# Low parts of 36 weights made by an accumulating transfer instead of a subtraction on VectorE

## The chip, the cores and the metric

The kernel runs on one core of a Trainium2 chip. The metric is the device time of one execution in microseconds; the median of three runs of the kernel before is 1605.04 us (1604.93 to 1605.2). TensorE multiplies, VectorE and ScalarE do elementwise work, GpSimd (POOL in the profile) does some of it too, and SyncE (SP) issues the transfers. Each engine works through its own instructions in order.

## The reference

One layer of an encoder, applied to two sequences of 512 tokens, model width 1024. In outline:

```python
def _layer(x, mem, l, p):
    xn = _rmsnorm(x, p['norm_mix'][l])
    mn = _rmsnorm(mem, p['norm_mem'][l])
    h = xn @ p['w_in'][l]
    u, q, k, v, xq, g = jnp.split(h, IN_SPLITS, axis=-1)
    y_s5 = _s5_branch(u, ...)                       # state-space recurrence, both directions, then a GLU
    y_diff = _diff_attention(rope(q), rope(k), v, lam, ...)
    y_x = _cross_attention(xq, mk, mv)              # mk, mv = split(mn @ w_mem_kv)
    branches = (y_s5, y_diff, y_x)
    merged = sum(sigmoid(g[..., n]) * (branches[n] @ p['w_up'][l, n]) for n in range(3))
    x = x + merged @ p['w_out'][l]
    xn2 = _rmsnorm(x, p['norm_ffn'][l])
    gate, up = jnp.split(xn2 @ p['w_ffn_in'][l], 2, axis=-1)
    return x + (silu(gate) * up) @ p['w_ffn_out'][l]
```

The columns of `w_in` are, in tiles of 128: 4 for `u`, 4 for `q`, 4 for `k`, 4 for `v`, 4 for `xq`, and 24 for the three gates `g` (8 each).

## The kernel before

**Products.** Operands are float32 numbers split in two: a high part rounded to fp32r and a low part, what is left of it. A product is three matmuls, high by high, high by low and low by high, accumulated in one PSUM bank (`mm3`, L153). A weight tile is 128 output columns by 1024 inputs, held as 128 partitions by 1024 elements (512 KB). For both sequences it is used in 2 x 8 x 3 = 48 matmuls of 512 columns each.

**A weight's way.** `weight` (L143) loads the tile to `wf`, then calls `split` (L131): ScalarE copies `wf` to `wh`, which rounds it, and VectorE subtracts `wh` from `wf` and writes `wl`. The pool `wp` (L83) has two buffers each of `wf`, `wh` and `wl`. So the load of a weight waits until the split of the weight two places earlier has read its `wf`, and the split waits until TensorE has finished with the `wh` and `wl` of the weight two places earlier.

**Who calls it.** `proj` (L163) multiplies a whole weight tile at once. It makes 18 of the 24 gates (`gates`, L402; three calls with the counts in `NG`, L42, and single ones between the steps of the recurrence) and the GLU's four products, whose weights are half as long (`nk` is 4). `units` (L614) is the same as a generator that gives control back every six matmuls; it makes the other six gates (`gate_units`, L627), the four queries to the memory (`xq_units`, L661), four queries and four keys of the differential attention (`qk_units`, L763, and one in the list at L686), and the merge's products, again with half-size weights. The values come from `v_units` (L637), which holds two weights at once and uses them in turn until its end.

**Order.** First the memory's keys and values and the norms; then the four `u` weights; then gates, which fill TensorE while S5's operands are made and while the recurrence runs on VectorE (`s5_gen`, L1410; `next(s5)` runs it a stretch further); the GLU; then attention on the memory, and the differential attention. In both attentions TensorE's order is the program's own (`PE.on`, L687): `fill` (L598) takes projections from a list (L686, L828) and puts their matmuls between the scores and the outputs. Then the merge, the output product, and the feed-forward part with its own weight preparation. Weights for the last product are prepared during the attentions: POOL makes sums of raw tiles (`raw_sums`, L451), ScalarE and VectorE split them, and SP stores them. In the rotation of queries and keys (`rotated`, L745) POOL has two of the steps. Outside the stretches with `PE.on`, and on the other engines, a planner orders each engine's instructions by a simulated time line (L1788). Three kinds of edges guide it without a wait at run time: `queued` puts transfers behind the last weight load (`last_w`), `behind` puts matmuls behind the last one (`last_mm`), and `issue_after(last_s[...])` puts VectorE's or ScalarE's instructions behind the last split of a weight (`last_s`); the last is used for the recurrence's stretches between the gates.

Of the kernel before, what the change touches and what calls it, by code (L numbers as in the profile page):

```python
# [10 lines left out]
F32 = mybir.dt.float32  # L11
F32R = mybir.dt.float32r
I32 = mybir.dt.int32
AF = mybir.ActivationFunctionType
ALU = mybir.AluOpType
# [4 lines left out]
P = 128  # L20
L = 512
DM = 1024
KD = DM // P
# [49 lines left out]
def encoder(ctx: ExitStack, tc: tile.TileContext, a, out):  # L73
    nc = tc.nc
    V, S, PO, PE = nc.vector, nc.scalar, nc.gpsimd, InOrder(tc, nc.tensor)
# [30 lines left out]
    def slot(tag, shape=(P, NT), dt=F32, name="sl"):  # L106
        return pools[tag].tile(list(shape), dt, tag=tag, name=name)

    def bank(tag="mm"):
        return pools[tag].tile([P, 512], F32, tag=tag, name="bk" + tag)  # L110
# [20 lines left out]
    def split(hi, lo, src, scale=None):  # L131

        if scale is None:
            h = S.copy(hi, src)  # L134
            l_ = V.tensor_tensor(out=lo, in0=src, in1=hi.bitcast(F32), op=ALU.subtract)  # L135
        else:
            h = S.activation(out=hi, in_=src, func=AF.Copy, scale=scale)
            l_ = V.scalar_tensor_tensor(out=lo, in0=src, scalar=scale, in1=hi.bitcast(F32), op0=ALU.mult, op1=ALU.subtract)
        return h, l_

    last_w = last_s = None

    def weight(src, n=DM, tag=None):  # L143
        nonlocal last_w, last_s
        wf = wp.tile([P, DM], F32, tag="wf", name="wf")
        last_w = nc.sync.dma_start(wf[:, :n], src)
        wh, wl = (slot(tag, dt=F32R, name=n_) if tag else wp.tile([P, DM], F32R, tag=n_, name=n_) for n_ in ("wh", "wl"))
        last_s = split(wh[:, :n], wl[:, :n], wf[:, :n])
        return wh, wl

    last_mm = None
# [1 line left out]
    def mm3(outs, wh, wl, xs, k, nk):  # L153

        nonlocal last_mm
        ws = slice(k * P, (k + 1) * P)
        for s, (xh, xl) in enumerate(xs):
            PE.matmul(outs[s], wh[:, ws], xh, start=(k == 0), stop=False)
            PE.matmul(outs[s], wh[:, ws], xl, start=False, stop=False)
        for s, (xh, xl) in enumerate(xs):  # L160
            last_mm = PE.matmul(outs[s], wl[:, ws], xh, start=False, stop=(k == nk - 1))

    def proj(src, hi, lo, nk=KD, seqs=(0, 1)):  # L163


        wh, wl = weight(src, nk * P)
        outs = []
        for s in seqs:
            cs = slice(s * L, (s + 1) * L)
            outs.append(bank())  # L170
            for k in range(nk):
                mm3(outs[-1:], wh, wl, [(hi[k][:, cs], lo[k][:, cs])], k, nk)
        return outs
# [135 lines left out]
    wf = wp.tile([P, DM], F32, tag="wf", name="wf")  # L309
    wh, wl = (wp.tile([P, DM], F32R, tag=n_, name=n_) for n_ in ("wh", "wl"))  # L310
# [6 lines left out]
    mem_part(2)  # L317
    mem_part(3)
    mw.append(weight(a["w_mk"][1]))
    with queued():  # L320
        nc.sync.dma_start(ident, a["ident"])
    mem_k(0, mw[0])
    mw.append(weight(a["w_mk"][2]))
    with queued():
        next(s5)
# [76 lines left out]
    def gates(n):  # L402

        for _ in range(n):
            t = next(todo)
            o = proj(a["w_in"][20 + t], xh, xl)
            gt = slot("ld", name="gt")
            for s in range(NS):
                cs = slice(s * L, (s + 1) * L)
                S.activation(out=gt[:, cs], in_=o[s], func=AF.Tanh, scale=0.5)  # L410
            nc.sync.dma_start(gD[t], gt)
# [113 lines left out]
    for t in range(4):  # L525
        o = proj(a["w_glu"][t], zh, zl, 4)
        sg = slot("zt", name="sg")
        for s in range(NS):
            S.activation(out=sg[:, s * L : (s + 1) * L], in_=o[s], func=AF.Tanh, scale=0.5, bias=bh[:, t : t + 1])
        for s in range(NS):  # L530
            g_ = sg[:, s * L : (s + 1) * L].rearrange("p (j c) -> p j c", j=T)
            V.scalar_tensor_tensor(out=g_, in0=g_, scalar=1.0, in1=zs[t][:, :, s, :], op0=ALU.add, op1=ALU.mult)
        nc.sync.dma_start(bD[0, t], sg)
# [79 lines left out]

    def units(src, hi, lo, use, nk=KD):  # L614

        wh, wl = weight(src, nk * P)
        for s in range(NS):
            cs = slice(s * L, (s + 1) * L)
            o = bank()
            for k in range(nk):  # L620
                mm3([o], wh, wl, [(hi[k][:, cs], lo[k][:, cs])], k, nk)
                if k == nk - 1:
                    use(s, o)
                if k % 2 == 1:
                    yield 6

    def gate_units():  # L627
        t = next(todo)
        gt = slot("ld", name="gt")

        def use(s, o):
            S.activation(out=gt[:, s * L : (s + 1) * L], in_=o, func=AF.Tanh, scale=0.5)

        yield from units(a["w_in"][20 + t], xh, xl, use)
        nc.sync.dma_start(gD[t], gt)
# [25 lines left out]
    def xq_units(h):  # L661
        def use(s, o):
            qs[h, s] = tuple(xa.tile([P, L], F32R, tag=n_, name=n_, bufs=3) for n_ in ("qh", "ql"))
            qs_in[:] = split(*qs[h, s], o)

        return units(a["w_in"][16 + h], xh, xl, use)
# [17 lines left out]
    V.tensor_tensor(out=nlam, in0=nlam, in1=le[:, 0:1], op=ALU.subtract)  # L684
    xq = {h: xq_units(h) for h in range(1, 4)}
    queue += [xq[1], gate_units(), xq[2], xq[3], v_units(0, v0), gate_units(), units(a["w_in"][4], xh, xl, dq0.__setitem__)]  # L686
    PE.on = True  # L687
    steps = [(h, s, lt) for h in range(4) for s in range(NS) for lt in range(4)]
# [214 lines left out]
    n = len(steps)  # L903
# [342 lines left out]
    for v, (m, lo_, hi_) in enumerate(VISITS):  # L1246
        ps = [bank() for _ in range(6)] + [aux()]
        for p in range(lo_, hi_):
# [12 lines left out]
            for p_, (nm, o) in zip(ps, SEVEN):  # L1261
                wh, wl = w[nm]
# [529 lines left out]
```

## Time and profile before

| what | us |
|---|---|
| median of the runs | 1605.04 (1604.93 to 1605.2) |
| profiled execution, span | 1603.0 |
| TensorE (PE) busy | 1587.1, 99% of the span |
| VectorE (DVE) busy | 1162.9, 73% |
| ScalarE (ACT) busy | 640.0, 40% |
| GpSimd (POOL) busy | 541.6, 34% |
| `wl<-wf,wh` on VectorE, all weights | 145.1 (134 instructions) |

The profile is of one execution. It gives the span from the first to the last instruction, 1603.0 us; a run's time as a whole isn't given beside it, and the median of the runs is 2.0 us longer. In rows of the time line the first number is the start in us from the span's start, the second the duration in us, then the engine, the line and the instruction with its tiles, and in brackets how long the engine stood idle before it and who released it. Matmuls overlap: each has a duration of about 0.39 us in the records, but in a steady run one starts every 0.23 us. So the time that 48 of them take is read from starts, not from durations.

The stages lie in the span as follows: `u` weights 50 to 97 us; gates beside S5 97 to 337, with the recurrence from 162 to 262; GLU to 371; both attentions to 706; merge, output and feed-forward to the end.

### The profile page before, as it was taken

Reading aid. Unit: us, or ns where it says so; the run is one execution under the profiler, and the core shown is the slowest. Engines: PE = TensorE matmul, PEld = TensorE weight load, DVE = VectorE, ACT = ScalarE, POOL = GpSimd, SP = SyncE. Lnnn points to the kernel's source line nnn. Section 1 sums busy time; section 2 is a strip of 40 time slices with the busy share of each in tenths; the row PEclk is TensorE's granted clock in tenths of the full one; section 3 lists DMA queues with packets and bytes.
Section 4 is the critical chain, followed back from the end, with each engine's and each line's share of the span. In section 5 each row is a group of like instructions: output and inputs, shape, how many; then the busy total and the mean of one; then the engine's idle time right before and its main releaser. Section 6 shows DMA issues by size and latency. Waiting matters only on the chain.

```text
span 1603.0 us, 21625 instructions
## 1 busy us (share of the span) xinstructions
PE 1587.1 (99%) x7838; PEld 1314.8 (82%) x7838; DVE 1162.9 (73%) x1856; ACT 640.0 (40%) x1142; POOL 541.6 (34%) x449
## 2 busy tenths in 40 slices
PE   9999999999999999999999999999999999999997
PEld 7888788888898778778878878888888888788877
DVE  7976996076773766776465678888898778988654
ACT  6544323274652455574133443332333323233323
POOL 0010100001333220300343367676665553444653
PEclk9999999999999999999999999999999999999998
DMA  9554523576762111244454432333323223986222
GB/s 366 173 160 150 179 95 125 180 273 201 252 224 102 54 47 40 73 156 140 145 190 132 144 118 80 131 119 129 121 106 118 79 88 119 344 332 198 80 66 106
DMA packets 104891, 237.86 MB, mean 148 GB/s; under 512 B 13520, under 2 KB 45008, under 8 KB 104784
## 3 DMA queue, kind: packets, MB, share of 16 engines
q1 hardware_dynamic: 104784, 236.47, 43.1%
q8 instruction: 62, 1.02, 0.3%
q14 instruction: 45, 0.37, 0.1%
HBM read 165.16 MB, written 71.27 MB: 147 GB/s over the span
## 4 chain that ended last, share of the span: by engine, by line
PE 87%; issue 4%; DVE 3%; DMA 3%; POOL 2%; ACT 0%; SPq 0%; POOLq 0%; DVEq 0%; ACTq 0%
PE bkmm L66 75%; PE bksc L66 3%; PE bktr L66 2%; PE bkoo L66 2%; PE bktr L69 2%; DVE tl L135 1%; PE bktr L1626 1%; POOL mg L793 1%; PE bktr L1597 1%; DMA yt<-bD 1%; PE bktr L1686 0%; PE bktr L1687 0%; PE bktr L1685 0%; PE bktr L1565 0%; DMA acc<-in_w_fo 0%
## 5 line engine op out<-in xcount | busy, mean ns | idle before, releaser
L66 PE MATMUL bkmm<-xh,wh 128*128 128x512 f32 x640 | 255.4, 399 | 0.0
L66 PE MATMUL bkmm<-xh,wl 128*128 128x512 f32 x640 | 250.9, 392 | 0.0
L66 PE MATMUL bkmm<-xl,wh 128*128 128x512 f32 x640 | 250.5, 391 | 0.0
L66 PE MATMUL bkmm<-tl,wh 128*128 128x512 f32 (+1 forms) x621 | 241.2, 388 | 1.4 <-DVE tl L135 1.4
L66 PE MATMUL bkmm<-th,wl 128*128 128x512 f32 (+1 forms) x621 | 241.0, 389 | 0.9 <-DVE wl L135 0.9
L66 PE MATMUL bkmm<-th,wh 128*128 128x512 f32 (+1 forms) x621 | 241.1, 389 | 0.0
L134 ACT CAST wh<-wf 128x1024 fp32r<-128x1024 f32 (+1 forms) x134 | 117.9, 880 | 224.1 <-PE bkmm L66 179.8
L135 DVE TENSOR_TENSOR wl<-wf,wh 128x1024 fp32r<-128x1024 f32 (+1 forms) x134 | 145.1, 1083 | 50.2 <-ACT wh L134 45.7
L66 PEld LDWEIGHTS bkmm<-xh,wh 128*128 128x128 f32 x640 | 120.3, 188 | 30.3 <-issue 7.9
L66 PE MATMUL bkmm<-th,w 128*128 128x512 f32 x432 | 141.5, 392 | 2.7 <-DVE up L1101 1.0
L66 PEld LDWEIGHTS bkmm<-xh,wl 128*128 128x128 f32 x640 | 120.2, 188 | 26.7 <-issue 1.3
L66 PEld LDWEIGHTS bkmm<-xl,wh 128*128 128x128 f32 x640 | 120.4, 188 | 22.4 <-issue 0.4
L66 PEld LDWEIGHTS bkmm<-tl,wh 128*128 128x128 f32 x621 | 116.6, 188 | 25.9 <-DVE tl L135 2.1
L66 PEld LDWEIGHTS bkmm<-th,wl 128*128 128x128 f32 x621 | 116.5, 188 | 25.7 <-DVE wl L135 1.7
L66 PEld LDWEIGHTS bkmm<-th,wh 128*128 128x128 f32 x621 | 116.6, 188 | 23.9
L1165 POOL TENSOR_TENSOR up<-up,acc 128x512 f32<-128x512 f32 x44 | 83.6, 1920 | 87.8 <-DVE up L1101 87.8
L454 POOL TENSOR_TENSOR raw<-raw 128x128 f32<-128x128 f32 x28 | 15.2, 545 | 284.4 <-DVE nb L545 206.5
L66 PEld LDWEIGHTS bkmm<-th,w 128*128 128x128 f32 x432 | 80.9, 188 | 23.8 <-DVE up L1101 3.4
L793 POOL TENSOR_TENSOR mg<-mg,gl 128x1024 f32<-128x1024 f32 x16 | 43.5, 2720 | 139.0 <-DVE gl L789 139.0
L548 ACT ACTIVATE e<-bksc,nb 128x512 f32<-128x512 f32 (+1 forms) x96 | 58.8, 615 | 73.5 <-DVE nb L543 51.9
L66 PE MATMUL bkmm<-tl,w 128*128 128x512 f32 x216 | 84.2, 390 | 0.0
L66 PE MATMUL bkmm<-yh,wh 128*128 128x512 f32 x192 | 75.9, 397 | 0.8 <-ACT wh L134 0.4
(641 smaller groups left out, 3527.8 us busy)
## 6 DMA issues: line engine op xcount, KB each, us to landing
wf<-in_w_in SPq DMA_DIRECT2D x40, 512.0 KB, 3.9
wD<-hl SPq DMA_DIRECT2D x28, 512.0 KB, 2.9
w<-wD SPq DMA_DIRECT2D x28, 512.0 KB, 5.0
gD<-gt SPq DMA_DIRECT2D x24, 512.0 KB, 2.8
gl<-gD SPq DMA_DIRECT2D x24, 512.0 KB, 3.4
wf<-in_w_fg SPq DMA_DIRECT2D x22, 512.0 KB, 3.7
wf<-in_w_fu SPq DMA_DIRECT2D x22, 512.0 KB, 3.6
aD<-ac SPq DMA_DIRECT2D x22, 512.0 KB, 3.1
```

Of the source, the lines that this page charges most:

```text
L66: return self.put(self.eng.matmul(*args, **kw))
L69: return self.put(self.eng.transpose(*args, **kw))
L134: h = S.copy(hi, src)
L135: l_ = V.tensor_tensor(out=lo, in0=src, in1=hi.bitcast(F32), op=ALU.subtract)
L454: PO.tensor_tensor(out=a22, in0=a21, in1=a22, op=ALU.add)
L548: last_x = S.activation(out=e, in_=sc, func=AF.Exp, bias=nb, scale=scale, accum_out=sm)
L793: PO.tensor_tensor(out=mg[m], in0=mg[m], in1=gt, op=ALU.add)
L1165: PO.tensor_tensor(out=up, in0=up, in1=accs[s], op=ALU.mult)
L1597: PE.matmul(kp[64 * hf : 64 * hf + 48, g * 144 : (g + 1) * 144], l_[:, 2 * hf + g, :], o_[:, 4 * g4 + 2 * hf + g, :], start=(l_ is lr48), ...
L1626: PE.matmul(ps[:, g * P : (g + 1) * P], w_[:, gg * P : (gg + 1) * P], u_[:, 8 * o + gg, :], start=True, stop=True)
```

## The change

A second way to split, `split_by_transfer`, is used for whole-length weights in `proj` and in `units`: 24 gates, four queries to the memory, four queries and four keys, 36 in all. ScalarE writes `wh` as before, and in a second pass writes the negated, rounded weight to `wl`. Then POOL issues a transfer that adds `wf` onto `wl` in place, reading and writing `wl` as float32. VectorE has no part in it. The four `u` weights, the values, the GLU's and the merge's weights are split as before. For the 36, `last_s` isn't set any more and stays at the last weight split in the old way.

```diff
+    def split_by_transfer(hi, lo, src):
+
+        S.copy(hi, src)
+        S.activation(out=lo, in_=src, func=AF.Copy, scale=-1.0)
+        return PO.dma_start(lo.bitcast(F32), src, accum_op=ALU.add)
+
     last_w = last_s = None
 
-    def weight(src, n=DM, tag=None):
+    def weight(src, n=DM, tag=None, far=False):
...
-        last_s = split(wh[:, :n], wl[:, :n], wf[:, :n])
+        if far:
+            split_by_transfer(wh, wl, wf)
+        else:
+            last_s = split(wh[:, :n], wl[:, :n], wf[:, :n])
         return wh, wl
...
     def proj(src, hi, lo, nk=KD, seqs=(0, 1)):
 
 
-        wh, wl = weight(src, nk * P)
+        wh, wl = weight(src, nk * P, far=nk == KD)
...
     def units(src, hi, lo, use, nk=KD):
 
-        wh, wl = weight(src, nk * P)
+        wh, wl = weight(src, nk * P, far=nk == KD)
```

## The prediction

> **What bounds the kernel now.** I read the core list first, then busy time and slices on the page, TensorE's waits, the windows by stage, and last the time line around each weight.
>
> ```profile
> core 0: 1603.0 us, clock 0.997
> PE 1587.1 (99%) x7838; PEld 1314.8 (82%) x7838; DVE 1162.9 (73%) x1856; ACT 640.0 (40%) x1142; POOL 541.6 (34%) x449
> ...
> 182.00:262.00 80.00, 80.00 (x370) 65.51 (x370) 76.70 (x212) 18.04 (x31) 0.50 (x2) 1.00 0.37 129
> 371.00:706.00 335.00, 335.00 (x1899) 277.50 (x1898) 226.13 (x484) 175.75 (x405) 80.98 (x96) 1.00 0.34 120
> 706.00:1603.00 897.00, 883.06 (x4043) 729.09 (x4041) 668.42 (x812) 301.63 (x447) 444.53 (x324) 0.99 0.42 141
> ```
>
> TensorE is the bound: busy 99% of the span at a granted clock of 0.997. In the windows (length, then busy time of PE, PEld, DVE, ACT, POOL, then clock, DMA share and GB/s) it is busy for the whole of the recurrence's 80 us and of attention's 335 us. The 36 weights of the change are cast between 97 and 671 us, all inside stretches of that kind. Asked who TensorE waited for between 42 and 706 us, the trace gives no row; over the whole span its longest are these:
>
> ```profile
> PE bkmm L66 <- DVE tl L135: 1.4, 2, 0.8
> ...
> PE bkmm L66 <- DVE up L1101: 1.0, 2, 0.7
> PE bkmm L66 <- DVE wl L135: 0.9, 1, 0.9
> ```
>
> So nothing that VectorE gives up in these stages can shorten them: there is no idle time of TensorE to remove. What the change can do is make TensorE wait, so the question is how late the low part may come.
>
> **What is removed, and what takes its place.** Removed: 36 subtractions `wl<-wf,wh` on VectorE. Added for each: a second pass on ScalarE (−hi), an accumulating transfer issued by POOL, and its landing. The rows for one weight in the recurrence, all shapes 128x1024:
>
> ```profile
> 239.32 1.05 ACT L134 CAST wh<-wf 128x1024 fp32r<-128x1024 f32 x1 [4.62 <-PE bkmm L66]
> 240.27 0.59 ACT L410 ACTIVATE gt<-bkmm 128x512 f32<-128x512 f32 x1
> 246.55 1.22 DVE L135 TENSOR_TENSOR wl<-wf,wh 128x1024 fp32r<-128x1024 f32 x1
> 250.68 0.39 PE L66 MATMUL bkmm<-xh,wl 128*128 128x512 f32 x1
> ```
>
> VectorE: 36 x 1.22 = 44 us of busy time go; worth 0 on the path, by the paragraph above. Even here, where the subtraction stood 6 us behind the recurrence's own steps, it ended 2.9 us before its first use.
>
> ScalarE: 36 passes more. A cast takes 1.05 us and the next instruction starts 0.95 us after it (239.32 to 240.27), so they add 36 x 0.95 = 34 us to an engine that is busy 18 us of 80 in the recurrence and 176 of 335 in attention. Behind the new pass stand the gates' tanh and, in attention, the exponentials and the casts of probabilities. I put that at 0, hidden by the depth with which scores are made ahead (L692). If that cover is gone, the 17 passes that fall in attention (without the queries of line 669) cost up to 17 x 0.95 = 16 us.
>
> The low part's path is now: cast (0.95), the second pass (1.05), then the transfer D from issue to landing. TensorE may read `wl` 2.0 + D after the cast's start. The cast waits for the buffer (two of each in `wp`), so it can't simply be moved ahead: in the row above it was released by TensorE, when the weight two places earlier had been used for the last time. What counts is therefore the room from the cast to the first matmul that reads `wl`. I took it for all 36. In the steady run of gates it is one weight's 48 matmuls, 250.68 − 239.32 = 11.36 us; seven gates have that. Two more have 381.79 − 371.72 = 10.07 and 337.44 − 326.62 = 10.82, and of the 23 others the shortest has 523.07 − 511.13 = 11.94:
>
> ```profile
> 326.62 1.04 ACT L134 CAST wh<-wf 128x1024 fp32r<-128x1024 f32 x1
> 337.44 0.39 PE L66 MATMUL bkmm<-xh,wl 128*128 128x512 f32 x1
> ...
> 371.72 1.04 ACT L134 CAST wh<-wf 128x1024 fp32r<-128x1024 f32 x1
> 381.79 0.39 PE L66 MATMUL bkmm<-xh,wl 128*128 128x512 f32 x1
> ...
> 511.13 1.05 ACT L134 CAST wh<-wf 128x1024 fp32r<-128x1024 f32 x1
> 523.07 0.39 PE L66 MATMUL bkmm<-xh,wl 128*128 128x512 f32 x1
> ```
>
> Four are tight: the first gate, behind the u weights; the first memory query, behind the half-size weights of the glu; the gate behind the first pair of value weights; and the last query behind the second pair.
>
> ```profile
> 96.98 1.06 ACT L134 CAST wh<-wf 128x1024 fp32r<-128x1024 f32 x1 [0.46 <-PE bkmm L66]
> 104.22 0.40 PE L66 MATMUL bkmm<-xh,wl 128*128 128x512 f32 x1
> ...
> 366.95 1.04 ACT L134 CAST wh<-wf 128x1024 fp32r<-128x1024 f32 x1
> 370.54 0.39 PE L66 MATMUL bkmm<-xh,wl 128*128 128x512 f32 x1
> ...
> 467.55 1.05 ACT L134 CAST wh<-wf 128x1024 fp32r<-128x1024 f32 x1 [0.33 <-PE bkmm L66]
> 473.00 0.39 PE L66 MATMUL bkmm<-xh,wl 128*128 128x512 f32 x1
> ...
> 633.25 1.05 ACT L134 CAST wh<-wf 128x1024 fp32r<-128x1024 f32 x1 [2.33 <-PE bkmm L66]
> 638.36 0.39 PE L66 MATMUL bkmm<-xh,wl 128*128 128x512 f32 x1
> ```
>
> Room: 7.24, 3.59, 5.45 and 5.11 us. The reason is the same each time: the weight two places earlier stayed in use until shortly before, because its partner is short (glu) or because both value weights are used in turn to the end.
>
> **What D is.** The kernel before has no POOL queue and no accumulating transfer, so it has to be bounded. Transfers of the same 512 KB:
>
> ```profile
> q1 hardware_dynamic: 104784, 236.47, 43.1%
> ...
> wf<-in_w_in SPq DMA_DIRECT2D x40, 512.0 KB, 3.9
> gD<-gt SPq DMA_DIRECT2D x24, 512.0 KB, 2.8
> fb<-aD SPq DMA_DIRECT2D x9, 512.0 KB, 6.2
> ...
> DMA to landing us min/median/max: 3.5/3.9/8.9
> ...
> 366.00:376.00 10.00, 10.00 (x46) 8.27 (x45) 6.42 (x8) 6.58 (x9) 0.00 (x0) 1.00 0.74 230
> 467.00:476.00 9.00, 9.00 (x61) 8.12 (x60) 7.41 (x19) 6.00 (x13) 2.70 (x4) 1.00 0.64 249
> ```
>
> (The row of three numbers is for the 40 loads from `w_in`.) From below: a plain store of that size, 2.8 us. From above: the slowest of the loads, 8.9 us. An accumulate reads two operands where a load reads one, and at two tight places the DMA engines are already busy 0.74 and 0.64 of the time. So I put it near the plain transfer that runs slowest in the median, 6.2, and take D = 6.0. Then `wl` is there 2.0 + 6.0 = 8.0 us after the cast's start, and TensorE waits for
>
> 8.0 − 3.59 = 4.4 (first query), 8.0 − 5.45 = 2.6 (gate), 8.0 − 5.11 = 2.9 (last query), 8.0 − 7.24 = 0.8 (first gate): 10.6 us in sum, with 32 weights covered.
>
> With D = 2.8 (4.8 after the cast) only the first query pays, 1.2 us; with D = 8.9 (10.9) the four pay 22.2 and two more 0.9, so 23.1 us.
>
> The Trainium skill, "DMA: Bandwidth & Descriptors", section "Anatomy of one DMA — SWDGE (gpsimd) path", fits a POOL-issued transfer as 2.0 us plus bytes over 436 GB/s; with two operands read (1 MiB) that would be an estimated 4.4 us, `wl` 6.4 us after the cast, 5.1 us of waiting in sum and 1610.1 us. No run here shows such a transfer yet.
>
> **The queues.** SP: the load of the weight after next waits for the buffer `wf`, until now for the subtraction, now for the landing. In the steady run that is no later (239.32 + 8.0 = 247.3, the subtraction ended 247.8). At the first gate it is 105.0 instead of 99.5; landed 3.5 to 8.9 us after that, by 113.9, it is in time for its cast.
>
> ```profile
> 99.48 0.64 SPq L146 DMA_DIRECT2D wf<-in_w_in  x1
> ...
> 115.98 1.06 ACT L134 CAST wh<-wf 128x1024 fp32r<-128x1024 f32 x1 [2.37 <-PE bkmm L66]
> ...
> 128.92 2.94 PE L1626 MATMUL bktr<-u__1212,wb 128*128 128x128 f32 x24
> ```
>
> Behind that load on SP stand S5's loads of `u`; TensorE first reads that tile at 128.9 us, 29 us later. I cost it at 0; if that cover were gone it is the 5 us of delay once. POOL: the issue waits for ScalarE's second pass, some 1 us or 2, and behind it stand the rotation's products and the sums for the last weights; TensorE never waited for POOL in these stages. The issue itself can be late on POOL, at one tight place where POOL is at work:
>
> ```profile
> 468.54 0.46 POOL L455 TENSOR_TENSOR raw<-raw 128x128 f32<-128x128 f32 x1
> 468.64 1.45 DVE L135 TENSOR_TENSOR wl<-wf,wh 128x1024 fp32r<-128x1024 f32 x1 [0.72 <-ACT wh L134]
> 469.08 1.32 POOL L456 TENSOR_TENSOR raw<-raw 128x128 f32<-128x128 f32 x1
> 470.48 0.46 POOL L457 TENSOR_TENSOR raw<-raw 128x128 f32<-128x128 f32 x1
> ```
>
> The second pass ends at 469.6 there and POOL is free at 470.9, so up to 1.4 us more for the gate; I keep it for the range.
>
> The order of all queues is planned anew with the changed instructions; `last_s` also stays at the u weights, so the recurrence's steps are no longer placed behind a gate's subtraction. As TensorE has no gap there, I cost both at 0.
>
> **Sum.** The profiled span of 1603.0 us stands 2.0 us under the median of the runs, 1605.04, and nothing outside the span changes: 1605.04 + 10.6 = 1615.6 us.
>
> **Rivals.** *Covered.* Within 0.2%, 3.2 us, is about what a measurement of this kernel can tell from no change. The waits sum to 3.2 us at 5.8 us after the cast, so D of 3.8 us or less, as the median load has it, gives "same": up to 1608.3. For it: plain stores take 2.8. Against it: twice the reading, and busy engines. Chance 0.13.
>
> *The steady run breaks.* Above 11.36 us after the cast, D over 9.3, each gate waits, not four weights: at 13 us after the cast the 36 rooms give 48.9 us (15 weights wait), 1654; at 12 they give 34.3, 1639. The mechanism is POOL being kept from its work: beside VectorE's subtraction, with both inputs in SBUF, the POOL sum above took 1.32 instead of 0.46 us, and in the recurrence VectorE runs such operations for 76.7 of 80 us. The DMA engines could also add two streams more slowly than they copy. Against it: a transfer has no POOL arithmetic in it, and 9.3 is above every load of a weight in `w_in`. Chance 0.20. On this the Trainium skill, "SBUF — State Buffer", section "SBUF: two separate sides", says that while VectorE runs an operation that takes both ports of the pair it shares with GpSimd, POOL-issued transfers are starved of descriptors, and that VectorE with two SBUF inputs shuts out GpSimd's reads. The row of 1.32 us agrees with the second; whether either reaches an issue, no run here shows.
>
> *Faster.* Planning anew could close gaps after 706 us, where TensorE is idle 897.0 − 883.1 = 13.9 us, mostly at the end. Of that, waits on VectorE are the 1.4 + 1.0 + 0.9 us quoted. If a VectorE that enters that stage less behind removed them all, and D were so short that no room is overrun (under 1.6), it is 1605.04 − 3.3 = 1601.7; the sign turns where D costs less than those waits are worth, at 3.3 us, D = 3.8. They lie behind the last changed weight. Chance 0.05.
>
> **How the numbers follow.** The forecast, waits at the tight places and a covered steady run (5.8 to 11.36 us after the cast, 3.3 to 25.9 us, 1608.3 to 1630.9), has 0.62; covered 0.13; steady run broken 0.20; faster 0.05. The range 1605 to 1640 leaves out the last and most of a broken steady run: faster 0.05, same 0.13, slower 0.82.
>
> **What would show it.** A POOL DMA queue with 36 issues of 512 KB, landing in 5 to 7 us; TensorE waiting for DMA `wl` at four places, longest at the first memory query (4 us); no wait in the run of gates from 206 to 261 us; VectorE's busy time about 44 us lower and ScalarE's 35 us higher. Wrong it would be if TensorE waits for `wl` once per gate (broken), if there is no such wait (covered), or if the waits are for `e`, `th` or `pH`, whose engines were held up by the new pass.

## The result, and the profile after

The changed kernel takes 1627.64 us (median of 3 runs, 1627.62 to 1627.74) where the kernel before takes 1605.04: a ratio of 1.0143, with a 95% interval of 1.0125 to 1.0161. It is 22.6 us slower. The forecast was 10.6 us slower, with a range that reached from 0 to 35.

The page of the changed kernel, its core list, busy times, the new queue and the new transfer (the last number of that line is the median from issue to landing, in us):

```profile
core 0: 1626.0 us, clock 0.993
PE 1594.3 (98%) x7838; PEld 1318.3 (81%) x7838; DVE 1126.3 (69%) x1820; ACT 672.5 (41%) x1178; POOL 566.6 (35%) x485
...
q0 software_dynamic: 5184, 18.88, 5.9%
...
wl<-wf POOLq DMA_DIRECT2D x36, 512.0 KB, 4.8
```

VectorE is 36.6 us less busy (1162.9 before), ScalarE 32.5 more (640.0 before). The new transfer lands in 4.8 us in the median, sooner than the 6.0 that the forecast had put in. And yet the loss is more than twice as large, so the sum must have missed a place. TensorE's waits of the changed kernel (total, times, longest):

```profile
PE bkmm L66 <- DMA wl<-wf: 9.6, 5, 5.5
...
PE bkmm L66 <- ACT sg L538: 2.4, 1, 2.4
...
PE bkoo L66 <- ACT xpTh L134: 2.0, 1, 2.0
...
PE bkmm L66 <- ACT wh L143: 0.8, 1, 0.8
...
PE bkoo L66 <- DVE nb L554: 0.6, 1, 0.6
```

None of these five rows is there before. Together they are 15.4 us, still not 22.6. To see where the time goes I laid the two traces side by side: for each of the 36 weights, the start of the first matmul that reads its low part, after minus before. This lag, in us, grows in steps, and each step is one place. (Up to the steady run it also falls again, from 3.2 to 0.6 us at 171 us, because S5's matmuls stand elsewhere in TensorE's order; from there on what is lost stays lost.) It was read in the same way from the later runs; "copies moved" and the other columns are the experiments below:

| place (start of that matmul before, us) | after | copies moved | four subtracted | plain transfer | eight subtracted |
|---|---|---|---|---|---|
| first gate (104.2) | 3.2 | 3.3 | 0.2 | 2.5 | 0.1 |
| steady run of gates (250.7) | 1.8 | 1.7 | 1.4 | 0.9 | 1.0 |
| behind the end of the recurrence (283.2) | 11.1 | 1.7 | 1.4 | 9.1 | 1.0 |
| first memory query (370.5) | 15.4 | 5.9 | 1.4 | 10.8 | 1.0 |
| second memory query (381.8) | 17.6 | 8.4 | 1.4 | 10.5 | 1.0 |
| last memory query (425.4) | 22.3 | 10.8 | 3.6 | 10.5 | 1.0 |
| gate behind the first value pair (473.0) | 23.4 | 12.4 | 4.5 | 11.1 | 1.0 |
| last gate (690.7) | 24.3 | 13.4 | 4.5 | 11.1 | 1.0 |

The spans differ by 1626.0 − 1603.0 = 23.0 us, so 1.3 of the 24.3 is won back after 706 us. The two largest steps that the forecast did not have are 9.3 us at the end of the recurrence and 4.7 us in memory attention: 14.0 us.

**The end of the recurrence.** ScalarE's time line before, from the cast of the gate that is due there:

```profile
250.20 1.06 ACT L134 CAST wh<-wf 128x1024 fp32r<-128x1024 f32 x1 [4.61 <-PE bkmm L66]
...
262.98 3.71 ACT L1677 COPY x<-st 64x2048 f32<-64x2048 f32 x2 [6.52 <-DVE st L1644]
266.60 1.04 ACT L134 CAST wh<-wf 128x1024 fp32r<-128x1024 f32 x1
```

The same stretch after, first ScalarE, then POOL, then TensorE:

```profile
258.67 3.72 ACT L1686 COPY x<-st 64x2048 f32<-64x2048 f32 x2 [15.01 <-DVE st L1653]
...
262.77 1.03 ACT L143 CAST wh<-wf 128x1024 fp32r<-128x1024 f32 x1
...
264.20 1.05 ACT L144 ACTIVATE wl<-wf 128x1024 fp32r<-128x1024 f32 x1
```

```profile
265.65 0.87 POOL L145 DMA_DIRECT2D wl<-wf  x1 [20.71 <-ACT wl L144]
```

```profile
263.86 0.50 PE L66 MATMUL bkmm<-xh,wh 128*128 128x512 f32 x1 [0.79 <-ACT wh L143]
264.19 0.40 PE L66 MATMUL bkmm<-xl,wh 128*128 128x512 f32 x1
270.12 0.80 PE L66 MATMUL bkmm<-xh,wl 128*128 128x512 f32 x1 [5.53 <-DMA wl<-wf]
270.71 0.63 PE L66 MATMUL bkmm<-xh,wh 128*128 128x512 f32 x1
...
275.36 0.40 PE L66 MATMUL bkmm<-xh,wl 128*128 128x512 f32 x1
```

Before, the cast of the gate (250.20) stands ahead of S5's copies `x<-st`, which wait for the last step of the recurrence. After, the copies stand ahead of the cast. ScalarE takes its instructions in order: it stands idle for 15.01 us until the recurrence ends, and the cast starts at 262.77 although nothing else held it (with the copies moved, in the first experiment, it starts at 251.94). From there the path is no longer than elsewhere: 270.1 − 262.8 = 7.4 us to the first use of `wl`. It is the start that was lost. Before, the same kind of delay met the weight behind it (cast at 266.60), which had 283.2 − 266.6 = 16.6 us of room.

The waits there are 0.8 + 5.5 = 6.3 us. Most of the other 3 us is in the last rows: behind the wait 12 matmuls start about 0.43 us apart (270.71 to 275.36) instead of 0.23. The lag is 8.6 us at the first of them that reads `wl` (270.12) and 11.1 at the next gate, so they cost 2.6 us. The windows of the changed kernel (after the five busy times: granted clock, DMA share, GB/s) show it as clock:

```profile
250.00:260.00 10.00, 10.00 (x46) 8.29 (x45) 9.37 (x25) 1.33 (x1) 0.00 (x0) 1.00 0.12 44
...
270.00:280.00 10.00, 9.88 (x33) 7.95 (x34) 0.00 (x0) 0.60 (x1) 0.00 (x0) 0.74 0.72 208
```

A window with 9.88 us of 10 busy is not a window at full speed: the third number from the right has to be read with it.

**Memory attention.** ScalarE's row of `hl` before, its time line after, and TensorE's row that waits for it:

```profile
408.97 0.53 ACT L137 ACTIVATE hl<-raw 128x384 fp32r<-128x384 f32 x1 [0.62 <-DMA wD<-hl]
```

```profile
429.74 0.53 ACT L137 ACTIVATE hl<-raw 128x384 fp32r<-128x384 f32 x1 [2.97 <-DMA wD<-hl]
430.17 0.35 ACT L134 CAST xpTh<-bktr 128x256 fp32r<-128x256 f32 x1
430.43 1.05 ACT L143 CAST wh<-wf 128x1024 fp32r<-128x1024 f32 x1
...
431.86 1.05 ACT L144 ACTIVATE wl<-wf 128x1024 fp32r<-128x1024 f32 x1
...
433.78 0.37 ACT L134 CAST xpTh<-bktr 128x256 fp32r<-128x256 f32 x1
```

```profile
434.20 0.50 PE L66 MATMUL bkoo<-xpTh,mkvh 128*128 128x512 f32 x1 [1.98 <-ACT xpTh L134]
```

The cast of probabilities that TensorE waits for stands behind a cast and a second pass, and all of them behind `hl`, which waited 2.97 us for its buffer (0.62 before): the store `wD<-hl` that empties it had not landed. `hl` starts 429.74 − 408.97 = 20.8 us later than before, 3.2 more than TensorE's lag of 17.6. `hl` is the high part of the feed-forward's output weight, which is split ahead of time in this stage; it has nothing to do with this attention but its place in ScalarE's queue. The issues between 405 and 445 us, first before, then after:

```profile
wD<-hl SPq DMA_DIRECT2D x6, 512.0 KB, 2.9
```

```profile
q0 software_dynamic: 384, 1.38, 17.6%
...
wD<-hl SPq DMA_DIRECT2D x6, 512.0 KB, 5.1
```

The stores land 2.2 us later, and the new queue takes 17.6% of the time of all DMA engines in that stretch. That looks like two streams that share the engines, but the rows of the store in question show something else. SP's waits from 417 to 423 us, its issues, and the stores from 422.2 to 433.2 us, where no transfer of the new queue is in flight:

```profile
SPq L152 <- DMA wl<-wf: 4.1, 1, 4.1
```

```profile
417.60 0.33 SPq L483 DMA_DIRECT2D wD<-hl  x1
422.12 0.33 SPq L152 DMA_DIRECT2D wf<-in_w_v  x1
...
424.79 0.49 SPq L483 DMA_DIRECT2D wD<-hl  x1
```

```profile
wD<-hl SPq DMA_DIRECT2D x2, 512.0 KB, 5.3
```

A weight's load waits on SP until `wl<-wf` has landed and its `wf` is free. Behind it on SP stand the stores; when it goes, they go close behind, and they land slowly (5.3 us) beside that load although nothing of the new queue runs. The store that `hl` waited for is the one of 424.79. So there are three things to tell apart: the order on ScalarE, the transfers and what waits for their landing, and the clock behind a wait.

### The profile page after: what moved, and what is told of

Read it like the earlier page. It is cut to its first block, busy times and chain, and to the rows that moved or that the text cites. A ratio compares the mean times of both kernels' runs of the same rounds, so it can differ in the third digit from the quotient of the medians.

```text
span 1626.0 us, 21711 instructions
## 1 busy us (share of the span) xinstructions
PE 1594.3 (98%) x7838; PEld 1318.3 (81%) x7838; DVE 1126.3 (69%) x1820; ACT 672.5 (41%) x1178; POOL 566.6 (35%) x485
## 3 DMA queue, kind: packets, MB, share of 16 engines
q0 software_dynamic: 5184, 18.88, 5.9%
q8 instruction: 62, 1.02, 0.3%
## 4 chain that ended last, share of the span: by engine, by line
PE 77%; issue 8%; DVE 5%; DMA 5%; POOL 2%; ACT 1%; SPq 0%; POOLq 0%; DVEq 0%; ACTq 0%
PE bkmm L66 68%; PE bktr L66 2%; DVE tl L135 2%; PE bksc L66 2%; DMA wl<-wf 2%; PE bkoo L66 1%; PE bktr L69 1%; DMA wD<-hl 1%; PE bktr L1635 1%; POOL mg L802 1%; PE bktr L1606 0%; DMA acc<-in_w_fo 0%; PE bktr L1696 0%; PE bktr L1695 0%; PE bktr L1694 0%
## 5 line engine op out<-in xcount | busy, mean ns | idle before, releaser
L66 PEld LDWEIGHTS bkmm<-xh,wl 128*128 128x128 f32 x640 | 121.6, 190 | 38.5 <-DMA wl<-wf 12.3
L134 ACT CAST wh<-wf 128x512 fp32r<-128x512 f32 (+1 forms) x98 | 80.1, 818 | 151.1 <-PE bkmm L66 111.3
L145 POOL DMA_DIRECT2D wl<-wf x36 | 32.1, 891 | 298.3 <-ACT wl L144 178.8
L135 DVE TENSOR_TENSOR wl<-wf,wh 128x512 fp32r<-128x512 f32 (+1 forms) x98 | 102.1, 1041 | 5.2 <-ACT wh L134 5.1
```

Source lines behind the costliest of these rows:

```text
L66: return self.put(self.eng.matmul(*args, **kw))
L145: return PO.dma_start(lo.bitcast(F32), src, accum_op=ALU.add)
```

## Experiments

The first four ran on one chip, with the kernel before at 1603.0 us (1602.03 to 1604.39); the last two on another chip with the kernel before at 1604.52 us (1602.84 to 1606.42). Times are compared as ratios to these.

**S5's copies kept behind the gate's second pass.** One edge is added to the order, nothing else.

```diff
+        n_ = S.activation(out=lo, in_=src, func=AF.Copy, scale=-1.0)
...
+            last_f = split_by_transfer(wh, wl, wf)
...
         gates(n)
-        with behind():
+        with behind(), tc.issue_after(last_f.ins):
             next(s5)
```

> One edge is added: on ScalarE, the copies of the recurrence's result into x stand behind the second pass of the last gate's weight instead of ahead of its cast. Nothing else moves: ScalarE's order differs from the changed kernel in these few places only. Theory 1 (the order of ScalarE at the end of the recurrence cost the largest part): TensorE's wait at 264 us (5.5 us for the transfer, 0.8 us for the cast) goes, and the 12 matmuls at half clock behind it; 9 us less than the changed kernel, about 1618.5. Theory 2 (the landing of the transfers is what costs, wherever the cast stands): the wait at that place stays, 1627 as the changed kernel.

Measured: 1616.61 us (1614.57 to 1617.27), ratio 1.0082 (1.0067 to 1.0097). ScalarE's time line and TensorE's longest wait for `wl`:

```profile
251.94 1.06 ACT L143 CAST wh<-wf 128x1024 fp32r<-128x1024 f32 x1 [4.66 <-PE bkmm L66]
...
258.81 3.71 ACT L1687 COPY x<-st 64x2048 f32<-64x2048 f32 x2 [4.38 <-DVE st L1654]
```

```profile
PE bkmm L66 <- DMA wl<-wf: 3.8, 4, 1.7
```

The cast starts at 251.94, the copies as early as in the changed kernel, and the whole step of 9.3 us is gone (lag 1.7 at 283.2). Of 0.0143 the ratio loses 0.0061, which is 9.8 us of 1605. The largest single piece of the loss was the place of two copies in an engine's queue.

**The second pass kept, VectorE adds in place of the transfer.** What does the pass cost without a transfer? As an instruction changes its engine, the planner orders all engines anew.

```diff
-        return PO.dma_start(lo.bitcast(F32), src, accum_op=ALU.add)
+        return V.tensor_tensor(out=lo, in0=src, in1=lo.bitcast(F32), op=ALU.add)
```

> ScalarE's second pass stays, and VectorE adds the weight to it in place of the POOL transfer, so the low part is there about 3.2 us after the cast begins. Theory 1 (order of ScalarE, and its doubled passes at the first memory query): part of the cost stays though no transfer is left; between 1607 and 1622, with a wait for the glu's tanh in front of the first memory query. Theory 2 (the landing is what costs): nothing is left, 1605 within 3 us.

Measured: 1614.64 us (1613.05 to 1618.76), ratio 1.0076 (1.0060 to 1.0091). TensorE's longest wait, and VectorE's row at the longest of the five places:

```profile
PE bkmm L66 <- DVE wl L145: 7.2, 5, 2.5
```

```profile
267.27 1.23 DVE L145 TENSOR_TENSOR wl<-wf,wl 128x1024 fp32r<-128x1024 f32 x1
```

This doesn't settle what it was meant to settle. The loss is 12 us (0.0076 of 1605), but in other places: four of the five waits are in the recurrence (229 to 269 us, the longest 2.5), where the addition stands on VectorE behind the recurrence's steps, and here behind its copies `x<-st`. On ScalarE the copies came to stand behind the gate's pass in this order. The lag is 8.8 us from the second memory query to the last, so with the passes and no transfer the step in memory attention is absent. Otherwise it shows only that a low part made in two steps on two engines has no reserve there, whoever takes the second step.

**The four tight weights subtracted as before.** With the moved copies; the other 32 keep the transfer, and the order is planned anew.

```diff
+TIGHT = (0, 18, 23, 32)
...
+        n_far += far
-        if far:
+        if far and n_far - 1 not in TIGHT:
```

> The edge of the first experiment, and the four weights with the least room (first gate, first memory query, the gate behind the first pair of values, the last query) are split by VectorE's subtraction as before; 32 weights keep the transfer. Theory 1: 22.6 less 9.3 (end of the recurrence), 6.4 (first memory query), 1.8 (first gate) and 1.9 (the other two) leaves the 4.7 us of the attention on the memory: 1609, or 1605 if the stall there goes with the new order. Theory 2 in its form 'each transfer costs its share': 32 of 36 weights keep 20 of the 22.6 us, 1625.

Measured: 1608.16 us (1607.07 to 1611.09), ratio 1.0034 (1.0022 to 1.0045). The step at the first memory query, 8.4 − 1.7 = 6.7 us with the copies moved, goes to nothing, and what is left is a step of 3.1 from the second memory query to the gate behind the first value pair, and 1.4 before it. TensorE's waits (the lines are numbered one higher here):

```profile
PE bkmm L67 <- DMA wl<-wf: 1.2, 1, 1.2
...
PE bkoo L67 <- ACT xpTh L135: 1.1, 1, 1.1
```

So the step at the first memory query belongs to that weight, and the step in memory attention does not hang on the four. At the first gate little is won: its own wait is gone, but 1.4 us stand in the steady run as well, and the wait of 1.2 us is for another transfer, near 208 us.

**A plain transfer of the same bytes.** The order of all engines is that of the changed kernel.

```diff
-        return PO.dma_start(lo.bitcast(F32), src, accum_op=ALU.add)
+        return PO.dma_start(lo.bitcast(F32), src)
```

> The transfer copies the weight over the negated high part instead of adding it (the low part is then wrong: it holds the whole weight); all instructions and their order are those of the changed kernel. It measures what the accumulation itself costs: a landing of 4.8 us in the median with it. If the second operand's reading is what it costs beside a plain transfer, 1 to 1.5 us less, 3.3 to 3.8, and the waits for wl shrink by that at each of the five places, 1621 to 1624; if the fixed cost of a POOL issue rules, the landing stays at 4.5 to 4.8 and the time at 1627.

Measured: 1615.53 us in one run, 1.0078 of the kernel before. The transfer's rows, first in the changed kernel, then here (POOL's issue in ns, least, median and most; then landing in us):

```profile
L145 POOL DMA_DIRECT2D wl<-wf x36: 850/875/1357, 99.7 to 697.6; - x36
DMA to landing us min/median/max: 4.4/4.8/8.8
```

```profile
L145 POOL DMA_DIRECT2D wl<-wf x36: 527/532/714, 99.9 to 684.4; - x36
DMA to landing us min/median/max: 2.8/3.5/7.4
```

And its stretch from 405 to 445 us, where the second pass stands on ScalarE as in the changed kernel:

```profile
wD<-hl SPq DMA_DIRECT2D x7, 512.0 KB, 3.8
```

SP's wait for the same load's buffer (408 to 413 us here), and the new queue over the whole kernel:

```profile
SPq L152 <- DMA wl<-wf: 2.7, 1, 2.7
```

```profile
q0 software_dynamic: 5184, 18.88, 2.9%
```

Adding in place costs 1.3 us of landing and 0.34 us of POOL for each transfer. Its packets also hold the DMA engines twice as long: 5.9% of their time in the changed kernel for the 5184 that take 2.9% here. I had expected a gain of 4 to 7 us, from the five waits for `wl`; it is about 10. In the lag, 6.2 us at the memory queries become 1.2 (10.5 − 9.3, where 9.3 is the lag at the last gate ahead of them; the shorter path brings no half clock behind it), and the whole step of 4.7 in memory attention goes as well (10.5 at the last memory query as at the second). The passes and their order are all still there. So the passes alone do not cause that step. SP is held 2.7 us for the landing instead of 4.1.

**Eight weights subtracted: the four, and the four others of memory attention.** The list of the third experiment becomes `TIGHT = (0, 18, 19, 20, 21, 22, 23, 32)`, and the order is planned anew.

> The kernel of the four subtracted weights and the moved copies, and beside them the four further weights that are made during memory attention (the second memory query to the last one) subtracted by VectorE as well; 28 weights keep the transfer. Theory (the accumulating transfers of this stage load the DMA engines, the stores and loads between the cast of the probabilities and their transposes land later, 5.1 instead of 2.9 us, and ScalarE's queue stands still behind them): the wait for the transposed probabilities near 416 us goes, the stage's transfers land in about 3 us again, TensorE's lag behind the kernel before at the gate behind the first value pair falls from 4.5 to about 1.5 us, and the time is about 1605 us (two to three under the four-weight kernel). Rival (ScalarE's queue is late because of its own passes and the order planned anew for the whole stage, not because of the transfers): part of the wait stays, the lag stays above 3 us, the time stays at 1607 to 1608 us.

Measured: 1606.54 us (1604.47 to 1607.51), ratio 1.0009 (0.9999 to 1.0018). Its stretch from 405 to 445 us:

```profile
wD<-hl SPq DMA_DIRECT2D x6, 512.0 KB, 3.1
```

The stores land in 3.1 us again and the step is gone: the lag is 1.0 us from 218 us to the last gate, and from 371 to 706 us TensorE waits for nothing, as before the change. This run takes both the transfers and the passes of that stage away; the plain transfer kept the passes and their order and had no such step either. The two together leave the adding transfers as its cause. Whether they act through SP's queue, as the rows near 424 us say, or also as traffic on the DMA engines, no run separates. What the other 28 cost can hardly be told from nothing (0.0009, with zero in the interval), and they bring nothing: TensorE never waited for the 28 subtractions that VectorE is spared.

**The wait filled with matmuls.** 28 extra matmuls stand ahead of the first matmuls of the gate at the end of the recurrence; the order of the other engines is that of the changed kernel.

```diff
             outs.append(bank())
+            for _ in range(28 if fill and s == 0 else 0):
+                PE.matmul(outs[-1], hi[0][:, 0:P], hi[0][:, cs], start=True, stop=True)
...
-            o = proj(a["w_in"][20 + t], xh, xl)
+            o = proj(a["w_in"][20 + t], xh, xl, fill=t == 12)
```

> The changed kernel with 28 extra matmuls (28 x 0.23 = 6.3 us at full clock) ahead of the first matmuls of the one gate at the end of the recurrence where TensorE stood still for 0.8 and 5.5 us; they write a bank that the gate then starts afresh, and the order of every engine is otherwise that of the changed kernel. Theory (some 2.5 us of the 9.3 us lost there are not waiting but the matmuls after it, which ran 0.43 instead of 0.23 us apart because TensorE had stood idle): the extra matmuls cost nothing, the matmuls behind them run 0.23 us apart, TensorE's lag at the next gate falls from 11.1 to about 8.6 us, and the time is 1624 to 1626 us beside 1627.6. Rival (the slow matmuls have another reason, as the transfers or the fresh weights): they stay 0.43 us apart and the time stays, or rises by up to 6 us if the extra matmuls add to the wait.

Measured: 1626.98 us (1624.95 to 1629.67), ratio 1.0139 (1.0124 to 1.0155). TensorE's time line, the window behind it, and an earlier wait of the same execution:

```profile
267.06 6.51 PE L66 MATMUL bkmm<-xh 128*128 128x512 f32 x28
273.41 0.39 PE L66 MATMUL bkmm<-xh,wh 128*128 128x512 f32 x1
...
274.09 0.39 PE L66 MATMUL bkmm<-xh,wh 128*128 128x512 f32 x1
```

```profile
270.00:280.00 10.00, 10.00 (x46) 8.28 (x45) 0.00 (x0) 0.60 (x1) 0.84 (x1) 1.00 0.79 211
```

```profile
211.79 0.50 PE L66 MATMUL bkmm<-xh,wl 128*128 128x512 f32 x1 [1.88 <-DMA wl<-wf]
```

Of the theory, this much holds: behind the extra matmuls, where TensorE did not stand idle, the others start 0.23 us apart at a clock of 1.00, beside the same fresh weight and with the DMA engines as busy (share 0.79, and 0.72 in the changed kernel). So it is the wait that brings the half clock.

That filling it pays does not show, neither in the time nor at the place: the lag at the next gate is 12.3 us, not 8.6 as expected. In the profiled execution the filling was too long. TensorE came to this gate at 267.06 instead of 262.9, because it was already 5.95 us late, not 1.8; the transfer was issued at 266.04 and landed 4.7 us later, at 270.8; the extra matmuls ran until 273.4. The gate costs 12.30 − 5.95 = 6.35 us, which is 28 x 0.227, and 2.6 of that lie behind the landing, as much as the half clock had cost. TensorE came late because near 209 us a transfer landed only after 10 us (the two of that stretch took 10.4 in the median), TensorE waited 1.9 us, and ran at half clock behind that wait too. Whether the other three runs lost their gain in the same way, the trace of one can't tell.

## Why the prediction was right or wrong

The sign and the range were right, and so was the reason as far as it went: the low part comes later than its room at a few places. The size was less than half of what came, and the larger part of the loss has other reasons. Step by step, with the lag at each place:

| step of the forecast | forecast, us | measured, us |
|---|---|---|
| first gate | 0.8 | 3.2 at once; 1.8 in the steady run, with other causes in it |
| first memory query | 4.4 | 4.0, and 2.2 more at half clock behind it |
| gate behind the first value pair | 2.6 | 1.1 |
| last query | 2.9 | 0.7 |
| order planned anew (end of the recurrence) | 0 | 9.3 |
| engines and queues beside it (memory attention) | 0 | 4.7 |

**The room and the path.** The way to reckon was right: lateness = path − room, to within two tenths. At the first memory query the cast starts at 378.25 and the low part is first read at 385.90, a path of 7.65 us, less 3.59 of room is 4.06; the lag grew by 4.0 from the last gate ahead of it (11.4). (TensorE's row names `sg` for 2.4 us of it. The order had put the next two hi matmuls ahead of the first `wl` one, and those wait for a bank that `sg` reads; without that wait the one for `wl` would have been so much longer.) The forecast path of 8.0 was made of wrong pieces that cancel: the landing is shorter (4.8, not 6.0), but POOL's issue starts 3.0 us after the cast and not 2.0, since a tanh stands between the two passes and 0.4 us pass before the issue. At the first gate the transfer, issued at 99.67, was waited for until 107.37, 7.7 us and not 6.0, with the DMA engines fully busy (share 1.02 from 100 to 105 us). At the two others the order put the pass ahead of the cast, so the path was 6.7 and 6.0 us, and the lateness 6.7 − 5.45 = 1.2 and 6.0 − 5.11 = 0.9. Where they arise, the four came to 3.2 + 4.0 + 1.1 + 0.7 = 9.0 us, for 10.7 in the forecast. The 3.2 did not last: 1.8 stand in the steady run, and with this weight subtracted still 1.4 and 1.0 (third and fifth experiment), so as far as these say, less than 1 us of it hangs on the first gate in the end.

**The step that failed** stands in the part on the queues: "The order of all queues is planned anew with the changed instructions ... As TensorE has no gap there, I cost both at 0." That TensorE has no gap says that nothing can be won there. It doesn't say that nothing can be lost. The two halves of that sentence differ: a kernel whose `last_s` follows the second pass gets the same order from the planner on every engine, so it wasn't `last_s` (that kernel was only planned, not run). It was the order itself, as the first experiment shows with 9.3 us. Why the copies came to stand ahead of the gate, I can only argue: the recurrence, relieved of the gates' subtractions, ends earlier (the copies start at 258.67 instead of 262.98), so that the work VectorE gave up pulled up what ScalarE must wait for.

**The second step that failed** is SP's queue: "the load of the weight after next waits for the buffer `wf`, until now for the subtraction, now for the landing. In the steady run that is no later". That cost nothing where it was reckoned, in the steady run and at the first gate. Memory attention was left out, where SP also carries the stores `wD<-hl`. There SP stood 4.1 us for a landing, the stores behind it went late and landed slowly (those of 512 KB in 5.1 us instead of 2.9), then came `hl` on ScalarE, then the cast of probabilities, then TensorE: 4.7 us. (The step depends on how the stage falls: with the copies moved it is 2.4.) The chain from SP on is read from the rows; shown by experiment is that the adding transfers cause the step. The other zero, for ScalarE's passes ("I put that at 0, hidden by the depth with which scores are made ahead"), was right, as the plain transfer shows.

**A term that was missing everywhere** is the clock behind a wait: 2.6 us on 6.3 of waiting at the end of the recurrence, about 2.2 on 3.1 at the first memory query, part of the 4.7 in memory attention.

**The rivals.** *Covered* is out: at 6.0 to 10.5 us, the path overran all four rooms. *The steady run breaks* was rightly the smaller chance and is nearer than it looks: two transfers near 201 and 212 us landed in 8.8 and 7.0 us in the changed kernel, the first 0.05 us before its use, and in 10.8 and 10.1 in the run with the filled wait, where TensorE waited 1.9 us. POOL had issued them in 0.88 us as elsewhere; it is the landing that was slow, and S5's load `c_n<-cD` beside them took 7.5 and 9.3 us too. In the changed kernel POOL started each issue within a microsecond of the second pass's end, and in the recurrence within 0.5, so the starving of POOL's transfers of which the Trainium skill writes ("SBUF — State Buffer", section "SBUF: two separate sides") does not show in the issues, although VectorE was busy for 9.4 us of 10 in the recurrence (250 to 260 us). Whether its operations there are of the kind that the page means, no run here shows. *Faster* is out; the eight-weight kernel, where nearly all of the loss is gone, isn't faster either.

**What would show it.** POOL's queue with 36 issues: yes. Landing in 5 to 7 us: a little less, 4.8. Waits for `wl` at four places: five, and the longest not at the first memory query but at the end of the recurrence, just behind the stretch (206 to 261) that I had named free of waits, and which was. ScalarE 35 us more: 32.5. VectorE 44 us less: the rows `wl<-wf,wh` lost 43.0 (145.1 to 102.1), the busy time only 36.6, in which neighbouring instructions whose records overlap count once.

## What to carry to other kernels

Where the bounding engine has no gap, a change that relieves another engine can only lose, and what it loses is where the order is tight: ask of each engine's queue what would stand ahead of the new chain, and compare the two orders before costing a re-planned one at zero. A new transfer is paid twice, by its own path against its room, and by whatever stands in a queue behind an instruction that waits for its landing; reckon both in every stage, not only where the path is tight. And a wait of some two microseconds on TensorE may not be over when it ends: depending on where it falls, the matmuls behind it run at half clock.

## What the runs showed of the hardware

**Half clock behind short waits.** In the changed kernel and the one with the filled wait, waits of 1.9 (209 us), 2.0 (432 us), 2.4 (382 us) and 5.5 us (264 us) were each followed by matmuls 0.43 us apart; one of 1.74 us (105 us) was not, at a clock of 1.00. Nor was a longer one, in the second experiment, behind which matmuls start 0.23 us apart:

```profile
268.55 0.50 PE L66 MATMUL bkmm<-xh,wl 128*128 128x512 f32 x1 [2.47 <-DVE wl L145]
```

So the length alone does not decide. In the filled-wait run the slow stretch behind the wait of 1.9 us begins about a microsecond after TensorE had started again and lasts from 212.83 to 216.24, 3.4 us: eight matmuls instead of fifteen, 8 x 0.2 = 1.6 us lost. The record of the granted clock in the eight traces has only slow stretches of 3.41 and 6.83 us between the first matmuls and the last, and within an execution they start on one grid of 3.413 us: in the filled-wait run at 212.82, 386.90 and 438.10, which is 51 and 15 steps apart. Laid over the waits, the grid orders them. The 1.88 us lie in one step (209.41 to 212.82), and the next step is slow. The 2.47 us are cut at 267.66 into 1.58 and 0.89, and neither next step is slow. Between the two the rows do not decide: 1.74 us in one step (104.63 to 108.04, changed kernel) was not followed by a slow one, 1.64 (1382.12 to 1385.53, third experiment) was. The Trainium skill, "TensorE: Matmul & The Clock Gate", section "What's actually happening", gives half clock after at least one idle window of about 3.4 us, windows that run freely. The length of 3.4 us and the free grid agree; but here 1.9 us without matmuls in a window was enough, so by these rows a window need not be idle throughout, only about the half of it.

**The price of adding in a transfer.** For 512 KB from SBUF onto SBUF, issued by POOL: 4.8 us to landing when it adds and 3.5 when it copies, 0.88 and 0.53 us of POOL, and twice the time on the DMA engines for each packet. The estimate that the prediction worked out from the fit in the Trainium skill, "DMA: Bandwidth & Descriptors", section "Anatomy of one DMA — SWDGE (gpsimd) path", with two operands read, was 4.4 us; the quickest of the 36 took just that, and the slowest 8.8.
